# Twelve weight-sum transfers moved to later, the order of compression, norm and scores, and a one-column product in front of each run of scores

## The chip, the cores and the metric

The kernel runs on one core of a Trainium2 chip. The metric is the device time of one execution in microseconds. A core has a matrix engine (PE, with its weight loads PEld), a vector engine (DVE), a scalar engine (ACT), a general engine (POOL) and a queue engine for transfers (SP). SP and POOL start the DMA transfers here: SP those that bring weights on the chip, POOL those of which the change moves twelve.

## The reference

One layer of a hybrid decoder, 256 positions, model width 2048, everything fp32. Three mixers work side by side on one projection; the attention shares queries between a compressed, a selected and a window branch.

```python
h = rms_norm(x, norm_mix_pre)
a_in, b_in, q, kv, nsa_g, merge_g = split(h @ w_in)          # 2048 x 13872
y_a = silu(layer_norm(causal_conv31(a * sigmoid(g)))) @ w_a_out
y_b = (u * (tril(W_s) @ layer_norm(v) + b)) @ w_b_out        # chunks of 128
kc = silu(blocks(k_cmp) @ w1_k) @ w2_k                       # 15 blocks, the same for vc
o = g0 * softmax(q @ kc) @ vc + g1 * softmax(q @ k_slc) @ v_slc + g2 * softmax(q @ k_win) @ v_win
y_c = o @ w_c_out                                            # 16 heads of 64
g_a, g_b, g_c = split(sigmoid(merge_g))
x = x + rms_norm((g_a * y_a + g_b * y_b + g_c * y_c) @ w_o, norm_mix_post)
u_g, u_v = split(causal_conv3(rms_norm(x, norm_ffn_pre) @ w_up))   # 2 x 5632
x = x + rms_norm((silu(u_g) * u_v) @ w_down, norm_ffn_post)
```

With 256 positions there are four key blocks, so the selected branch takes all of them, and the window of 512 masks nothing but the future: both are causal attention over all positions, with keys and values of their own.

## The kernel before, in words

All weights stream from memory, most as pieces of 512 KB. `fetch` starts a piece's transfer on SP into one of five buffers `wraw`. `piece` then splits it: ACT writes the rounded part `whi` (line 199), DVE the rest `wlo` (line 200), four buffers each. A product with such weights is three products, `hi`·`hi`, `hi`·`lo` and `lo`·`hi` (lines 249 to 251 in `mm_t`; lines 228 and 235 for the feature-major projections; line 1056 in class `Seven`).

The order of the program is: projections `a`, `b`, `c` and `q`; `branch()`, which for each of four column blocks `cb` of 512 columns forms gates `pg` from eight pieces of `wt_g` and then the product `py` from four pieces of `wt_p`, and leaves `mac`; `outs_a()`, the same for the first mixer (product `py`, result `ya`); gates and output in `Seven`, which replaces seven of eight products by sums of weights; and the FFN, whose loop also uses sums.

The sums of weights are made in memory by transfers that POOL starts, `ahead`: copies and additions between DRAM buffers. The list `steps` holds them in order. `ahead_by(mark, n)` copies one column of a result of the main line into `tick`, so POOL waits for that result, and then starts the next `n` steps:

```python
        pooled(G.tensor_copy, tick, mark)
        for dst, src, how in steps[:n]:
            pooled(G.dma_start, dst, src, **how)
        del steps[:n]
```

Whatever `n` leaves over, later calls take; the FFN loop spreads what is left over its 42 passes.

Smaller work stands in generators in a queue `bg`: the norm of the first mixer (`lna_gen`, `lnz_gen`: lines 601 to 606, tiles `lz`, `lg`, `At`), the compression of keys and values (`cmp_prep`, `cmp_gen`: `bk`, `zp`, `zs`, `hp`; w1 comes as four pieces for each of the two), and the attention (`cmp_attn` and eight `Unit`s: scores `s` at line 854, weights, transposes `pp`, products into `O`, result `Ct`, whose rest is line 933). `pump(ns)` runs this queue for a budget of nanoseconds between parts of the main line; `hold("outputs")` lets the compression begin at the second block of gates. `in_turn` takes one step of each of its generators in turn, `apart` doubles what a step counts for, and `until(name)` runs the queue to a mark.

Products write to PSUM: four banks hold the main line's results, and four the generators', handed out in turn by `bank`. A run of scores fills two banks, one for each half of the 128 rows (64 rows a head), and takes the halves alternately; `in_turns` makes each product follow the one before it on PE, though others may come between. These products are fp32, and the trace has two records for each.

A scheduler with a simulated timeline of its own sets the final order on every engine, within `tc.issue_after` (this one after that one) and `tc.high_priority` (this one earlier than its place in the program).

Of the kernel before, what the change touches and what calls it, by code (L numbers as in the profile page):

```python
# [64 lines left out]
def block(ctx: ExitStack, tc: tile.TileContext, x, xf, x0, fp, cst, rows, sgw, w1, w2, wf_a, wt_bv, wf_bu, wf_c,  # L65
# [688 lines left out]
        while name not in marks:  # L754
            yield debt[0]

    for kv in range(2):
        bg.append(cmp_prep(kv))
        if kv == 0:
            bg.append(hold("outputs"))  # L760
        bg.append(cmp_gen(kv))

    kkv = s8([128, 2, 1024], F32, "kkv")
    kk = kkv[:, 0].rearrange("p (g b t) -> p g b t", g=2, b=2)
    for i in range(4):
        pc = ftile(wf_c[4 + i], hT)
        fsum(pc, kk[:, i % 2, i // 2], rb=rb)
        ahead_by(kk[:, i % 2, i // 2, 0:1], 1)
        pump(BUDGET)
    vsw = kkv[:, 1].rearrange("p (t c) -> p t c", t=2)  # L770
    gsg = P1.tile([128, 2, 48], F32, name="gsg")
# [22 lines left out]
    for i in range(8):  # L794
        pq = ftile(wf_q[i], hT)
        fsum(pq, qf[:, i], scale=0.125, rb=rb)
        ahead_by(qf[:, i, 0:1], 2 + i % 2)
        pump(BUDGET)


# [2 lines left out]
    def apart(work):  # L803

        for ns in work:
            yield 2.0 * ns
# [39 lines left out]
    def in_turns(work):  # L846


        last = None
        for out, lhsT, rhs, start, stop in work:  # L850
            with ExitStack() as order:
                if last is not None:
                    order.enter_context(tc.issue_after(last))
                last = PE.matmul(out, lhsT=lhsT, rhs=rhs, start=start, stop=stop, skip_group_check=True).ins  # L854

    half = [slice(0, 64), slice(64, 128)]

    class Unit:
# [8 lines left out]
        def scores(self):  # L867
            qt, gg, br = self.at
            nk = (qt + 1) * 128
            mk = cs[:, K_MK + 256 - nk:K_MK + 256]  # L870
            hpb = 512 // nk
            ep = s8([128, 2, 4, 256], F32, f"ep{self.nm}")
            e = self.e = [ep[:, r] for r in range(2)]
            m = self.m = P1.tile([128, 2, 8], F32, tag="am", bufs=2, name="am" + self.nm)
            for b in range(4 // hpb):
                ps = [bank([128, hpb, nk], f"s{self.nm}{b}{r}") for r in range(2)]
                in_turns([(ps[r][:, jj], qf[half[r], gg * 4 + b * hpb + jj, qt * 128:qt * 128 + 128],
                           kk[half[r], gg, br, 0:nk], True, True) for jj in range(hpb) for r in (1, 0)])
                for jj in range(hpb):
                    j = b * hpb + jj  # L880
                    for r in range(2):
                        V.tensor_tensor_reduce(e[r][:, j, 0:nk], ps[r][:, jj], mk, 1.0, -3e38, ALU.add, ALU.max,
                                               m[:, r, j:j + 1])
                        yield nk * 1.05 + 130
            V.tensor_scalar(m[:, :, 0:4], m[:, :, 0:4], -1.0, None, op0=ALU.mult)
# [92 lines left out]
    def attn():  # L978

        units = [Unit(qt, gg, br) for qt in (1, 0) for gg in range(2) for br in range(2)]  # L980
        yield from in_turn(lnz_gen(), apart(cmp_attn(1)), apart(units[0].scores()))
        marks.add("A")
        Ct_box["t"] = s16(P1, [128, 8, 2, T], R, "Ct")
        for n, u in enumerate(units):
            if n + 1 < len(units):
                if n == 1:
                    yield from in_turn(apart(cmp_attn(0)), units[n + 1].scores())
                else:
                    yield from units[n + 1].scores()
            if u.at[2] == 0:  # L990
                V.tensor_mul(spread, pct[u.at[0]][:, u.at[1]][:, None, :].to_broadcast([128, 4, 128]),
                             cs[:, K_RJ:K_RJ + 4][:, :, None].to_broadcast([128, 4, 128]))
            yield from u.weights()
            if SUMS_AT <= n < SUMS_AT + 4:
                yield from input_sums(n - SUMS_AT)
            if u.at[2] == 0:
                O = bank([128, 4, 128], "O" + u.nm)
            yield from u.values(O)
# [149 lines left out]
    def branch():  # L1148

        for cb in range(4):  # L1150
            pg = [PS.tile([128, 512], F32, tag="acc", name=f"pg0{cb}{t}") for t in range(2)]
            for q in range(4):
                hs = granule(wt_g[cb * 4 + q])
                for k in range(4 * q, 4 * q + 4):
                    hi, lo = hs[(k % 4) // 2]
                    c = slice((k % 2) * 512, (k % 2) * 512 + 512)
                    for t in range(2):
                        ts = slice(t * 128, t * 128 + 128)
                        with ExitStack() as order:
                            if (cb, k) == (1, 0):  # L1160
                                order.enter_context(tc.issue_after(norm["v"]))
                            mm_t(pg[t], hT[:, k, 0, ts], hT[:, k, 1, ts], hi[:, c], lo[:, c], k == 0, k == KT - 1)
                if (cb, q) == (0, 2):
                    until("m")
                    debt[0] = 0.0
                elif q < 3:
                    if (cb, q) == (1, 2):
                        marks.add("outputs")
                    pump(BUDGET)
            tgs = {}  # L1170
            for t in range(2):
                for a in range(2):
                    tgs[t, a] = q1(f"mg0{cb}{t}{a}")
                    with tc.high_priority(offset=int(PR)):
                        gated[0] = S.activation(tgs[t, a], pg[t][:, a * 256:a * 256 + 256], AF.Tanh,
                                                scale=rh[:, t:t + 1]).ins
            marks.add("gates")
            pump(BUDGET)
            py = [PS.tile([128, 512], F32, tag="acc", name=f"py0{cb}{t}") for t in range(2)]
            for q in range(2):  # L1180
                hs = granule(wt_p[cb * 2 + q])
                if cb == 0 and q == 0:
                    until("B")
                act = Bt_box["t"]
                for k in range(4 * q, 4 * q + 4):
                    hi, lo = hs[(k % 4) // 2]
                    c = slice((k % 2) * 512, (k % 2) * 512 + 512)
                    for t in range(2):
                        ts = slice(t * 128, t * 128 + 128)
                        with ExitStack() as order:  # L1190
                            if (cb, k) == (0, 7):
                                until("v")
                                debt[0] = max(debt[0], 0.0)
                                order.enter_context(tc.issue_after(norm["v"]))
                            pe_last[0] = mm_t(py[t], act[:, k, 0, ts], act[:, k, 1, ts], hi[:, c], lo[:, c], k == 0, k == 7)
                if q == 0:
                    pump(BUDGET)
            for t in range(2):
                for a in range(2):
                    cc = slice(cb * 512 + a * 256, cb * 512 + a * 256 + 256)  # L1200
                    y = mac[:, t, cc]
                    with tc.high_priority(offset=int(PR)):
                        V.scalar_tensor_tensor(y, tgs[t, a], 1.0, py[t][:, a * 256:a * 256 + 256], op0=ALU.add,
                                               op1=ALU.mult)
            ahead_by(mac[:, 0, cb * 512:cb * 512 + 1], (8, 8, 8, 8)[cb])
            pump(BUDGET)

    def outs_a():

        for cb in range(4):  # L1210
            py = [PS.tile([128, 512], F32, tag="acc", name=f"py1{cb}{t}") for t in range(2)]
            for q in range(2):
                hs = granule(wt_p[(4 + cb) * 2 + q])
                if cb == 0 and q == 0:
                    until("A")
                for k in range(4 * q, 4 * q + 4):
                    hi, lo = hs[(k % 4) // 2]
                    c = slice((k % 2) * 512, (k % 2) * 512 + 512)
                    for t in range(2):
                        ts = slice(t * 128, t * 128 + 128)  # L1220
                        pe_last[0] = mm_t(py[t], At[:, k, 0, ts], At[:, k, 1, ts], hi[:, c], lo[:, c], k == 0, k == 7)
                if q == 0:
                    pump(BUDGET)
            for t in range(2):
                with tc.high_priority(offset=int(PR)):
                    V.tensor_copy(ya[:, t, cb * 512:cb * 512 + 512], py[t])
            if cb < 2:
                ahead_by(ya[:, 0, cb * 512:cb * 512 + 1], (8, 4)[cb])
            pump(BUDGET)

    def m_sums(n):
# [772 lines left out]
```

## Time and the profile before

| | us |
|---|---|
| median of 3 runs | 1563.44 (1559.46 to 1569.31) |
| profiled execution, its own time | 1563.63 |
| its span in the trace | 1561.9 |
| PE busy | 1551.4 (99%) |
| DVE busy | 1322.3 (85%) |
| ACT busy | 970.2 (62%) |
| POOL busy | 220.9 (14%) |
| mean granted clock of PE | 0.998 |

Times below are microseconds from the start of the span. The gates of block 0 begin at about 302; `mac` of the four blocks is ready at 335.1, 377.5, 426.7 and 470.5, when POOL's `tick` copies run; the first two of `outs_a` follow at 495.8 and 517.6. A busy PE is not PE at its peak: the ends of products are modelled, and the distance from one product to the next tells more than the length of one.

### The profile page before, as it was taken

Reading aid. Unit: us, or ns where it says so; the run is one execution under the profiler, and the core shown is the slowest. Engines: PE = TensorE matmul, PEld = TensorE weight load, DVE = VectorE, ACT = ScalarE, POOL = GpSimd, SP = SyncE. Lnnn points to the kernel's source line nnn. Section 1 sums busy time; section 2 is a strip of 40 time slices with the busy share of each in tenths; the row PEclk is TensorE's granted clock in tenths of the full one; section 3 lists DMA queues with packets and bytes.
Section 4 is the critical chain, followed back from the end, with each engine's and each line's share of the span. In section 5 each row is a group of like instructions: output and inputs, shape, how many; then the busy total and the mean of one; then the engine's idle time right before and its main releaser. Section 6 shows DMA issues by size and latency. Waiting matters only on the chain.

```text
span 1561.9 us, 23350 instructions
## 1 busy us (share of the span) xinstructions
PE 1551.4 (99%) x8101; PEld 1315.6 (84%) x8101; DVE 1322.3 (85%) x2233; ACT 970.2 (62%) x1536; POOL 220.9 (14%) x349
## 2 busy tenths in 40 slices
PE   9999999999999999999999999999999999999998
PEld 8888889887777778888888888888888888888887
DVE  7899999876766579978886898888888887899898
ACT  7644454455677776656665766566666666577774
POOL 1011351221102100000000032222222221100000
PEclk9999999999999999999999999999999999999999
DMA  9687998999779867777774699999999999989896
GB/s 369 195 268 234 273 300 246 296 303 288 236 215 256 223 230 262 247 227 259 268 256 164 205 301 309 306 335 290 287 280 283 282 284 281 316 287 346 313 375 218
DMA packets 130711, 426.13 MB, mean 273 GB/s; under 512 B 15008, under 2 KB 16784, under 8 KB 129824
## 3 DMA queue, kind: packets, MB, share of 16 engines
q1 hardware_dynamic: 99648, 329.46, 60.2%
q0 software_dynamic: 30368, 94.52, 25.7%
q8 instruction: 63, 1.03, 0.3%
q10 hardware_dynamic: 576, 0.66, 0.1%
q14 instruction: 56, 0.46, 0.1%
HBM read 416.45 MB, written 90.44 MB: 325 GB/s over the span
## 4 chain that ended last, share of the span: by engine, by line
PE 97%; DMA 1%; DVE 1%; ACT 1%; issue 0%; DVEq 0%; ACTq 0%
PE ps L228 29%; PE ps L235 15%; PE pg L1056 8%; PE pd1a L1056 4%; PE pd0b L1056 4%; PE pd0a L1056 3%; PE pd1b L1056 3%; PE py L250 3%; PE py L251 3%; PE py L249 3%; PE poa L1056 2%; PE pg L251 1%; PE pg L250 1%; PE pg L249 1%; PE s L854 1%; PE po L249 1%
## 5 line engine op out<-in xcount | busy, mean ns | idle before, releaser
L200 DVE TENSOR_TENSOR wlo<-wraw,whi 128x1024 fp32r<-128x1024 f32 (+1 forms) x344 | 418.2, 1221 | 92.3 <-ACT whi L199 73.3
L199 ACT ACTIVATE whi<-wraw 128x1024 fp32r<-128x1024 f32 (+1 forms) x344 | 361.8, 1057 | 212.0 <-PE ps L228 117.8
L228 PE MATMUL ps<-h2T,whi 128*128 128x512 f32 x1360 | 317.2, 390 | 0.0
L228 PEld LDWEIGHTS ps<-h2T,whi 128*128 128x128 f32 x1360 | 252.4, 188 | 50.4
L235 PEld LDWEIGHTS ps<-h2T,wlo 128*128 128x128 f32 x1360 | 169.4, 192 | 3.6
L235 PE MATMUL ps<-h2T,wlo 128*128 128x256 f32 x1360 | 170.7, 283 | 0.0
L228 PE MATMUL ps<-hT,whi 128*128 128x512 f32 x640 | 151.9, 390 | 0.0
L228 PEld LDWEIGHTS ps<-hT,whi 128*128 128x128 f32 x640 | 117.9, 188 | 23.0
L1012 DVE TENSOR_TENSOR wlowraw<-wraw,whiwraw 128x1024 fp32r<-128x1024 f32 x74 | 89.7, 1222 | 26.6 <-ACT whiwraw L1012 24.6
L556 DVE SCALAR_TENSOR_TENSOR cv<-hb,fps,cv 128x256 f32<-128x256 f32 x240 | 105.9, 491 | 0.1
L1012 ACT ACTIVATE whiwraw<-wraw 128x1024 fp32r<-128x1024 f32 x74 | 77.9, 1059 | 40.4 <-PE py L251 11.8
L1615 ACT ACTIVATE fa<-fs,fps 128x256 f32<-128x256 f32 x88 | 52.8, 600 | 54.1 <-DVE fs L274 52.3
L235 PEld LDWEIGHTS ps<-hT,wlo 128*128 128x128 f32 x640 | 81.1, 191 | 2.5
L235 PE MATMUL ps<-hT,wlo 128*128 128x256 f32 x640 | 82.8, 283 | 0.0
L1056 PE MATMUL pg<-whiwraw,hT 128*128 128x512 f32 x256 | 82.3, 395 | 0.0
L129 POOL DMA_DIRECT2D ahead<-in_wt_dq_dram x91 | 68.1, 901 | 87.1 <-DMA ahead<-in_wt_dq_dram 87.1
L129 POOL DMA_DIRECT2D ahead<-ahead x53 | 43.5, 822 | 245.4 <-DMA ahead<-in_wt_dq_dram 103.8
L271 ACT ACTIVATE t<-ps 128x256 f32<-128x256 f32 x125 | 47.5, 382 | 49.0 <-PE ps L235 26.3
L129 POOL COPY tick<-gh 128x1 f32<-128x1 f32 x44 | 37.5, 853 | 186.3 <-ACT gh L1623 186.3
L1056 PEld LDWEIGHTS pg<-whiwraw,hT 128*128 128x128 f32 x256 | 47.9, 188 | 10.4 <-issue 0.2
L1616 DVE SCALAR_TENSOR_TENSOR fa<-fs,fps,fa 128x255 f32<-128x255 f32 x88 | 42.4, 481 | 16.6 <-ACT fa L1615 16.5
L272 DVE TENSOR_TENSOR t<-ps,t 128x256 f32<-128x256 f32 x125 | 52.4, 420 | 0.5 <-ACT t L271 0.5
(2520 smaller groups left out, 3317.9 us busy)
## 6 DMA issues: line engine op xcount, KB each, us to landing
wraw<-in_wf_up_dram SPq DMA_DIRECT2D x176, 512.0 KB, 6.6
ahead<-in_wt_dq_dram POOLq DMA_DIRECT2D x74, 512.0 KB, 9.8
wraw<-in_wt_p_dram SPq DMA_DIRECT2D x48, 512.0 KB, 6.4
wraw<-in_wt_dq_dram SPq DMA_DIRECT2D x33, 512.0 KB, 6.0
wraw<-in_wf_a_dram SPq DMA_DIRECT2D x32, 512.0 KB, 5.1
ahead<-in_wt_gq_dram POOLq DMA_DIRECT2D x32, 512.0 KB, 9.9
wraw<-in_wt_g_dram SPq DMA_DIRECT2D x32, 512.0 KB, 7.1
wraw<-in_wt_gp_dram SPq DMA_DIRECT2D x32, 512.0 KB, 4.9
```

The source lines that it names most:

```text
L129: in_pool[:] = [op(*args, **kw).ins]
L199: S.activation(hi[:, :n], raw[:, :n], AF.Copy)
L200: V.tensor_sub(lo[:, :n], raw[:, :n], hi[:, :n].bitcast(F32))
L228: ins = PE.matmul(ps, lhsT=ws[k // 8][0][:, c:c + 128], rhs=mov[:, k], start=bool(k == 0 and first), stop=bool(k == n - 1 and not first), ...
L235: ins = PE.matmul(ps[:, 1], lhsT=ws[k // 8][1][:, c:c + 128], rhs=mov[:, k, 0], start=bool(k == 0 and not first), stop=bool(k == n - 1 and ...
L249: PE.matmul(ps, lhsT=xh, rhs=hi, start=first, stop=False)
L250: PE.matmul(ps, lhsT=xh, rhs=lo, start=False, stop=False)
L251: return PE.matmul(ps, lhsT=xl, rhs=hi, start=False, stop=last).ins
L556: V.scalar_tensor_tensor(ca[:, j], hb[:, j, k:k + T], w(j, k), ca[:, j], op0=ALU.mult, op1=ALU.add)
L1012: seq[eng] = [op(*args, **kw).ins]
L1056: ins = PE.matmul(bank, lhsT=a[x], rhs=w[y], start=first and j == 0, stop=bool(last and j == 2), skip_group_check=more).ins
L1615: S.activation(a, s, AF.Identity, bias=fps[:, C_FB + f:C_FB + f + 1], scale=w[2])
```

## The change

It has three parts.

1. The counts of `ahead_by` change. After each of the four `kk` projections none are started (before: 1 each); after the eight `q` projections 2 each (before: 2 and 3 alternately); after block 0 of `branch` 4 (before 8); in `outs_a` 8, 8 and 4 after the first three blocks (before 8 and 4 after the first two). By the end of block 0 twelve fewer have been started; `outs_a` takes up eight of them and the FFN loop four (108 there, before 104).
2. The second `cmp_gen` leaves the queue and is taken in turn with the norm and the scores of the first unit; `cmp_attn(1)`, which was in turn with these two, follows behind them.
3. In front of each run of scores stands a product of one column into the bank of half 0. It is written over by the run's own product. The banks are asked for in the other order, and the rest of the run follows it at high priority.

```diff
-    for kv in range(2):
-        bg.append(cmp_prep(kv))
-        if kv == 0:
-            bg.append(hold("outputs"))
-        bg.append(cmp_gen(kv))
+    bg.append(cmp_prep(0))
+    bg.append(hold("outputs"))
+    bg.append(cmp_gen(0))
+    bg.append(cmp_prep(1))
...
         fsum(pc, kk[:, i % 2, i // 2], rb=rb)
-        ahead_by(kk[:, i % 2, i // 2, 0:1], 1)
...
-        ahead_by(qf[:, i, 0:1], 2 + i % 2)
+        ahead_by(qf[:, i, 0:1], 2)
...
                 if last is not None:
                     order.enter_context(tc.issue_after(last))
+                    order.enter_context(tc.high_priority(offset=int(PR)))
...
-                ps = [bank([128, hpb, nk], f"s{self.nm}{b}{r}") for r in range(2)]
-                in_turns([(ps[r][:, jj], qf[half[r], gg * 4 + b * hpb + jj, qt * 128:qt * 128 + 128],
+                ps = [bank([128, hpb, nk], f"s{self.nm}{b}{r}") for r in (1, 0)][::-1]
+                in_turns([(ps[0][:, 0, 0:1], qf[half[0], gg * 4, 0:128], kk[half[0], gg, br, 0:1], True, True)]
+                         + [(ps[r][:, jj], qf[half[r], gg * 4 + b * hpb + jj, qt * 128:qt * 128 + 128],
                            kk[half[r], gg, br, 0:nk], True, True) for jj in range(hpb) for r in (1, 0)])
...
-        yield from in_turn(lnz_gen(), apart(cmp_attn(1)), apart(units[0].scores()))
+        yield from in_turn(cmp_gen(1), lnz_gen(), apart(units[0].scores()))
+        yield from cmp_attn(1)
...
-            ahead_by(mac[:, 0, cb * 512:cb * 512 + 1], (8, 8, 8, 8)[cb])
+            ahead_by(mac[:, 0, cb * 512:cb * 512 + 1], (4, 8, 8, 8)[cb])
...
-            if cb < 2:
-                ahead_by(ya[:, 0, cb * 512:cb * 512 + 1], (8, 4)[cb])
+            if cb < 3:
+                ahead_by(ya[:, 0, cb * 512:cb * 512 + 1], (8, 8, 4)[cb])
```

Three places in the order of instructions show what this moves. The numbers behind the names of tiles count buffers and differ between the two programs. First PE, at the last run of scores of a unit, before the change: `s` are the scores, `py` a product of the second mixer, `Bt` its operand.

```order
L251 MATMUL py_4348<-whi_4482,Bt 128x512
L854 MATMUL s_4401<-kkv,qf 128x256
L249 MATMUL py_4349<-whi_4482,Bt 128x512
L250 MATMUL py_4349<-wlo_4483,Bt 128x512
L251 MATMUL py_4349<-whi_4482,Bt 128x512
L854 MATMUL s_4400<-kkv,qf 128x256
L854 MATMUL s_4401<-kkv,qf 128x256
L854 MATMUL s_4400<-kkv,qf 128x256
```

One product of the run stands apart from its other three, with three 512-column products between them. The same engine after the change, at a run of the first units; line 853 is the line 854 of before, and `pcp` is the transpose in `cmp_attn`.

```order
L837 MATMUL pcp_4330<-idn,ce_4318 128x128 x2
L853 MATMUL s_4339<-kkv,qf 128x1
L853 MATMUL s_4338<-kkv,qf 128x256
L853 MATMUL s_4339<-kkv,qf 128x256
L853 MATMUL s_4338<-kkv,qf 128x256
L853 MATMUL s_4339<-kkv,qf 128x256
L853 MATMUL s_4350<-kkv,qf 128x1
```

The four products stand together behind their one-column product; so they do in all twelve runs, and the claim of the next run stands behind them here. Two of the twelve claims stand alone among 512-column products.

Second ACT, at the gates of block 2, before: the `whi` at line 199 are the splits of weight pieces.

```order
L694 ACTIVATE bk_3926<-bt_3942 128x4x64
L199 ACTIVATE whi_4043<-wraw_4041 128x1024
L199 ACTIVATE whi_4049<-wraw_4047 128x1024
L199 ACTIVATE whi_4079<-wraw_4077 128x1024
L199 ACTIVATE whi_4143<-wraw_4141 128x1024
L199 ACTIVATE whi_4149<-wraw_4147 128x1024
L199 ACTIVATE whi_4208<-wraw_4206 128x1024
L199 ACTIVATE whi_4214<-wraw_4212 128x1024
L716 ACTIVATE zs_4091<-zp_3947 128x256
L716 ACTIVATE zs_4092<-zp_3947 128x256
```

And the same stretch of ACT after the change.

```order
L199 ACTIVATE whi_4040<-wraw_4038 128x1024
L694 ACTIVATE bk_3910<-bt_3926 128x4x64
L603 ACTIVATE lg_3996<-lz_3995 128x256
L601 ACTIVATE lz_4027<-cv,fps 128x256
L603 ACTIVATE lg_4028<-lz_4027 128x256
L601 ACTIVATE lz_4088<-cv,fps 128x256
L199 ACTIVATE whi_4046<-wraw_4044 128x1024
L603 ACTIVATE lg_4089<-lz_4088 128x256
L601 ACTIVATE lz_4147<-cv,fps 128x256
L199 ACTIVATE whi_4076<-wraw_4074 128x1024
L605 ACTIVATE At<-lz_3995 128x256
L605 ACTIVATE At<-lz_4027 128x256
```

Norm operations (`lz`, `lg`, `At`) now stand among the splits; before, the norm came behind `zs`.

Third POOL, from the `tick` of block 0 of `branch` on, before: the `bt` are buffers of the compression.

```order
L129 COPY tick<-mac 128x1
L129 DMA ahead_80<-ahead_80 128x512
L129 DMA ahead_81<-in_wt_gq_dram 128x512
L129 DMA ahead_81<-in_wt_gq_dram 128x1024
L129 DMA ahead_82<-in_wt_gq_dram 128x1024
L687 MEMSET bt_3589 128x16
L687 MEMSET bt_3594 128x16
L687 MEMSET bt_3599 128x16
L687 MEMSET bt_3604 128x16
L129 DMA ahead_81<-ahead_81 128x512
L129 DMA ahead_82<-in_wt_gq_dram 128x512
```

POOL after the change, from the second transfer behind the same `tick` to the `tick` of block 1.

```order
L129 DMA ahead_79<-in_wt_gq_dram 128x512
L129 DMA ahead_79<-in_wt_gq_dram 128x1024
L129 DMA ahead_80<-in_wt_gq_dram 128x1024
L687 MEMSET bt_3577 128x16
L687 MEMSET bt_3582 128x16
L687 MEMSET bt_3587 128x16
L687 MEMSET bt_3592 128x16
L687 MEMSET bt_3911 128x16
L687 MEMSET bt_3916 128x16
L687 MEMSET bt_3921 128x16
L687 MEMSET bt_3926 128x16
L129 COPY tick<-mac 128x1
```

Of the eight transfers behind the first `tick` four are left, and the buffers of both compressions follow at once. The `tick` of block 1 has eight behind it before and after.

At the end of the attention, the last unit's product into `O` stood among the first products of `Seven` (`pg0s`); after the change it stands eleven products ahead of them.

## The prediction

> **What bounds the kernel now.** First the page: the span, the busy shares, the largest wait of the transfer queue, and the landing times of two weight streams.
>
> ```profile
> span 1561.9 us, 23350 instructions
> PE 1551.4 (99%) x8101; PEld 1315.6 (84%) x8101; DVE 1322.3 (85%) x2233; ACT 970.2 (62%) x1536; POOL 220.9 (14%) x349
> L129 POOL COPY tick<-gh 128x1 f32<-128x1 f32 x44 | 37.5, 853 | 186.3 <-ACT gh L1623 186.3
> wraw<-in_wt_p_dram SPq DMA_DIRECT2D x48, 512.0 KB, 6.4
> wraw<-in_wt_g_dram SPq DMA_DIRECT2D x32, 512.0 KB, 7.1
> ```
>
> PE is busy in 99% of the span. The diff takes no product away, so it can only gain where PE stands still or runs slowly. I therefore cut the span into stretches (columns: us, PE busy, PEld, DVE, ACT, POOL, granted clock, DMA share, GB/s).
>
> ```profile
> 300.00:320.00 20.00, 20.00 (x90) 16.56 (x89) 13.37 (x22) 8.78 (x9) 5.92 (x11) 1.00 1.03 319
> 360.00:380.00 20.00, 17.69 (x94) 14.53 (x95) 14.67 (x23) 15.29 (x23) 2.10 (x5) 1.00 0.87 312
> 380.00:400.00 20.00, 18.65 (x82) 15.19 (x82) 11.18 (x15) 8.40 (x12) 3.63 (x6) 0.91 0.99 296
> 395.50:398.80 3.30, 3.30 (x9) 2.62 (x8) 3.19 (x7) 3.06 (x5) 0.03 (x1) 0.50 1.11 324
> 400.00:560.00 160.00, 160.00 (x798) 119.47 (x798) 104.13 (x297) 119.20 (x303) 20.05 (x32) 1.00 0.79 225
> 560.00:580.00 20.00, 18.89 (x84) 13.41 (x84) 14.65 (x16) 13.07 (x16) 0.00 (x0) 1.00 0.60 188
> ```
>
> PE stands still for 2.31 us in 360 to 380, 1.35 in 380 to 400 and 1.11 in 560 to 580, and runs 3.3 us at half clock. Between 400 and 560 it never stops. The weight loads' waits name the places; first those of 340 to 400, last that of 540 to 600 (us in total, times, longest).
>
> ```profile
> PEld py L249 <- ACT whi L199: 2.1, 2, 1.1
> PEld hp L720 <- ACT zs L716: 1.8, 1, 1.8
> PEld py L250 <- DVE wlo L200: 1.0, 1, 1.0
> PEld pg L250 <- DVE wlo L200: 1.0, 1, 1.0
> PEld pg0s L1056 <- DVE Ct L933: 1.5, 1, 1.5
> ```
>
> A weight load waits while the product before it still streams, so each wait costs PE a product's pitch less. That pitch is 389.74 to 389.96, taken as 0.23 us:
>
> ```profile
> 389.74 0.39 PE L251 MATMUL pg<-whi,hT 128*128 128x512 f32 x1
> 389.96 0.39 PE L249 MATMUL pg<-whi,hT 128*128 128x512 f32 x1
> 393.51 1.16 PE L720 MATMUL hp<-sel,zs 128*128 128x64 f32 x8 [1.35 <-ACT zs L716]
> 396.35 0.63 PE L249 MATMUL pg<-whi,hT 128*128 128x512 f32 x1
> 396.77 0.63 PE L250 MATMUL pg<-wlo,hT 128*128 128x512 f32 x1
> ```
>
> - **A**, `py` of column block 1 (blocks count from 0) waiting for split weights: 2.1 + 1.0 - 3 x 0.23 = 2.4 us.
> - **B**, `pg` for `wlo`: 1.0 - 0.23 = 0.8.
> - **C**, `hp` for `zs`: 1.8 - 0.23 = 1.6. Behind it the clock halves: the pitch is 0.42 (396.35 to 396.77), so the 3.3 us hold the work of 3.3 x 0.23 / 0.42 = 1.8 and lose 1.5; with the edges I take 1.7.
> - **D**, the first lump behind attention for `Ct`: 1.5 - 0.23 = 1.3.
>
> Together 7.8 us, 0.5% of the span.
>
> **The change part by part.** *Fewer transfers before 400 us.* The chain of the first two rows gives the late weight pieces; the others are POOL's issues beside them.
>
> ```profile
> 352.94 9.74 DMA wraw<-in_wt_p_dram
> 380.87 11.16 DMA wraw<-in_wt_g_dram
> 350.38 0.81 POOL L129 DMA_DIRECT2D ahead<-ahead  x1 [7.37 <-issue]
> 352.92 0.80 POOL L129 DMA_DIRECT2D ahead<-in_wt_oq_dram  x1
> 378.94 2.00 POOL L129 DMA_DIRECT2D ahead<-in_wt_oq_dram  x3
> ```
>
> The `wt_p` piece takes 9.74 us against a median of 6.4, and starts with POOL's transfers of 350 to 353. These are the second four of column block 0's eight, which the change drops; the twelve that it has dropped by then also leave POOL less behind. I take A as gone: -2.4 (0 to -2.4). B's piece and C's come behind block 1's tick, whose eight stay, and the 11.16 us piece is issued 2 us behind three of them. The backlog that they meet is shorter, so I take half of B, -0.4, and two thirds of C, -1.0 (each from 0 to all). The half clock stands behind C's stop and a run of 64-column products, and goes if that stop is short: -1.3 (0 to -1.7).
>
> [...]
>
> *Later transfers.* Eight come back behind the second and third of `outs_a`'s blocks (about 495 to 555), four in the FFN. The nearest row is 300 to 320: DMA share 1.03, and PE still 20.00 of 20.00; 400 to 560 has 0.79. So 0, at worst another A: +2.4. In the FFN POOL's tick waits 186.3 us for `gh` in all; four more issues of 0.8 us fit there. Without that cover they would be 4 x 0.8 = 3.2 us of POOL, which no product waits for until the sums are read.
>
> *One-column products.* Score runs that are split cost more than whole ones:
>
> ```profile
> 404.81 0.70 PE L854 MATMUL s<-kkv,qf 64*128 64x256 f32 x2
> 405.43 0.50 PE L251 MATMUL pg<-whi,hT 128*128 128x512 f32 x1
> 407.47 1.13 PE L854 MATMUL s<-kkv,qf 64*128 64x256 f32 x6
> 408.52 0.50 PE L250 MATMUL pg<-wlo,hT 128*128 128x512 f32 x1
> 462.31 1.13 PE L854 MATMUL s<-kkv,qf 64*128 64x256 f32 x8
> 463.37 0.50 PE L251 MATMUL py<-whi,Bt 128*128 128x512 f32 x1
> ```
>
> Split: 0.62 + 1.05 = 1.67; whole: 1.06; difference 0.6. Six of the twelve runs are split in the order of before, and the pitches give 3.3 us in all; after the change all twelve stand whole: -3.3 (0 to -3.3, since some of that may only move). Each has a product of one column more, ten next to its run or other 64-row products, two alone. The nearest row has one-column products of 128 rows:
>
> ```profile
> 43.84 0.50 PE L436 MATMUL ssp<-ones,sq 128*128 128x1 f32 x4
> 44.20 0.49 PE L249 MATMUL pv<-swraw,hT 128*128 128x512 f32 x1
> ```
>
> Four records are two fp32 products, 0.36 us: 0.18 each, 12 x 0.18 = +2.2. The lower end is 0, since its one column may pass under the weight load of the next product; the upper end is the price of a whole product of the run, 1.06 / 4 = 0.27 each, 3.2. I take 0.18, a product of the same one column. The two alone cost a change to 64 rows and back, by the split run 0.6 / 3 = 0.2 each: +0.4. The step comes to -0.7, between -3.3 (claims and switches free) and +3.6 (dear claims, and no split saved).
>
> [...]
>
> *The order of compression, norm and scores.* The first norm operations now stand on ACT ahead of weight splits of block 2's gates (the order shown above), where before only splits stood.
>
> ```profile
> 382.36 1.06 ACT L199 ACTIVATE whi<-wraw 128x1024 fp32r<-128x1024 f32 x1 [2.58 <-PE pg L251]
> 388.81 1.06 ACT L199 ACTIVATE whi<-wraw 128x1024 fp32r<-128x1024 f32 x1 [5.39 <-PE pg L251]
> 392.13 1.06 ACT L199 ACTIVATE whi<-wraw 128x1024 fp32r<-128x1024 f32 x1 [2.25 <-DMA wraw<-in_wt_g_dram]
> 396.82 0.59 ACT L601 ACTIVATE lz<-cv,fps 128x256 f32<-128x256 f32 x1
> 399.25 0.42 ACT L605 ACTIVATE At<-lz 128x256 fp32r<-128x256 f32 x1 [0.33 <-DVE lz L604]
> ```
>
> Ten operations of 0.42 to 0.59 us are 4 x 0.5 + 2 x 0.5 + 4 x 0.42 = 4.7 us. They are covered by ACT's idle time in 380 to 393, 2.58 + 5.39 + 2.25 = 10.2 us. But they wait for DVE between one another, and the split behind them, and PE behind it, wait too. With full cover 0, without any 4.7, with a second half clock 6.4; nearest is the cover: I take **+1.5**. At the end of attention the last bank's product now stands 11 products (2.5 us) ahead of the first lump, where before it stood among them; D's 1.3 us fits: -1.1 (0 to -1.3).
>
> **Sum.** -2.4 - 0.4 - 1.0 - 1.3 - 1.1 - 0.7 + 1.5 = -5.4. From the profiled execution, 1563.63 us, which stands 0.2 above the median of the runs: **1558.2 us**.
>
> **Rivals.** *The burst behind block 1 decides.* C and the half clock hang on the eight transfers at 377 to 381 alone, which stay; for it speaks the 11.16 us row, against it the shorter backlog. Then B's -0.4, C's -1.0 and the clock's -1.3 are out: 1558.2 + 2.7 = 1560.9.
>
> *Slower: norm operations hold the splits.* The ten ACT operations queue in the stretch where PE has two pieces in hand. Decisive is that ACT's 10.2 us idle come in three pieces, each waiting for `pg` or a landing: if the operations fall outside them, 4.7 us reach PE, and the 1.7 of a second half clock. C and the half clock stay. Kept are A's -2.4, D's -1.1 and the -0.7: 1563.6 - 4.2 + 6.4 = 1565.8. Against it: the cover is twice the work.
>
> *The change doesn't relieve the queue.* `wt_p` at 352.94 is late through the compression's pieces and its own granules, not through POOL. For it: 300 to 320 holds a DMA share of 1.03 without a stop. Then A, B, C and the clock stay, -0.7 and -1.1 stand against +1.5: 1563.3.
>
> **How the numbers follow.** Forecast 0.45, burst 0.25, slower 0.14, no relief 0.13, anything else 0.03. The gains at their bounds (2.4 + 0.8 + 1.6 + 1.7 + 1.3 + 3.3) are 11.1, so the low end is 1552; the high end takes in the second rival and 1 us of the later transfers: 1567. A measurement here tells 1%, 15.6 us, from no change; all stops together are half of that, so faster by over 1% has 0.02, and slower by it, which needs more than the second rival's whole price, 0.03.
>
> **What would show it.** A right: between 355 and 370 no `py` waits for `whi` or `wlo`, and no `wt_p` piece takes over 8 us there. C right: `hp` waits less than 0.6 us and no stretch has 0.50. The claims right: each 64-row run whole, and a run of five products at most 1.3 us. Rival two shows as `pg` of block 2 waiting for `whi` with ACT busy on `lz`, `lg` or `At` just before. I am wrong if new stops of over 3 us stand in 400 to 560, where before there are none, or if the FFN waits for its sums.

## The result and the profile after

The changed kernel takes 1555.07 us (median of 8 executions, 1554.56 to 1556.31); the kernel before, measured beside it, 1566.56 (8 executions, 1559.46 to 1571.14). The ratio is 0.9933, with a 95% interval of 0.9915 to 0.9951: faster by 0.7%. The time lies inside the range of the prediction; the gain is about twice what was forecast from the profiled executions, of which more below. Two things changed at once: the median fell by 11.5 us, and the spread went from 11.7 us to 1.8.

The profiled execution after took 1556.31 us, 7.3 below the profiled one of before. First the page, with the rows that were shown of before.

```profile
span 1554.6 us, 23403 instructions
PE 1547.9 (100%) x8125; PEld 1316.0 (85%) x8125; DVE 1322.2 (85%) x2233; ACT 968.7 (62%) x1536; POOL 230.6 (15%) x346
wraw<-in_wt_p_dram SPq DMA_DIRECT2D x48, 512.0 KB, 6.1
wraw<-in_wt_g_dram SPq DMA_DIRECT2D x32, 512.0 KB, 6.1
```

PE has 24 more matmul records (two for each of the twelve claims) and is busy for 3.5 us less in a span that is 7.3 us shorter: it stands still 3.8 us less, and none of the stretches below runs at half clock. The same stretches as before (us, PE, PEld, DVE, ACT, POOL, granted clock, DMA share, GB/s):

```profile
360.00:380.00 20.00, 20.00 (x110) 16.93 (x109) 15.78 (x33) 16.25 (x31) 3.04 (x6) 1.00 0.77 238
380.00:400.00 20.00, 19.72 (x107) 16.37 (x105) 15.20 (x34) 13.57 (x27) 2.69 (x4) 1.00 1.03 321
400.00:560.00 160.00, 160.00 (x813) 119.40 (x812) 99.52 (x268) 113.54 (x285) 25.37 (x41) 1.00 0.83 240
560.00:580.00 20.00, 20.00 (x90) 16.52 (x89) 19.60 (x23) 14.90 (x17) 0.00 (x0) 1.00 0.86 286
```

The 2.31, 1.35 and 1.11 us of standing in 360 to 380, 380 to 400 and 560 to 580 are 0, 0.28 and 0, and the clock is 1.00 in all four. Weight loads that wait (first of 340 to 400, then of 400 to 600):

```profile
PEld hp L720 <- ACT zs L716: 0.7, 1, 0.7
PEld pg L1057 <- DVE Ct L933: 0.2, 1, 0.2
```

No `py` and no `pg` waits for `whi` or `wlo`. `hp` still waits 0.7 - 0.23 = 0.5 us for `zs`, and behind it the pitch is that of the full clock:

```profile
390.47 1.15 PE L720 MATMUL hp<-sel,zs 128*128 128x64 f32 x8 [0.28 <-ACT zs L716]
393.17 0.39 PE L251 MATMUL pg<-whi,hT 128*128 128x512 f32 x1
393.40 0.40 PE L250 MATMUL pg<-wlo,hT 128*128 128x512 f32 x1
```

POOL, from block 0's `tick` to block 1's, and then the transfers issued in 350 to 360, among them block 1's four `wt_p` pieces: the share of the DMA engines by queue, and the median time to landing.

```profile
335.55 0.18 POOL L129 COPY tick<-mac 128x1 f32<-128x1 f32 x1 [21.22 <-DVE mac L1204]
336.68 2.18 POOL L129 DMA_DIRECT2D ahead<-in_wt_gq_dram  x3
374.06 0.18 POOL L129 COPY tick<-mac 128x1 f32<-128x1 f32 x1 [6.06 <-DVE mac L1204]
...
q1 hardware_dynamic: 815, 2.97, 85.4%
wraw<-in_wt_p_dram SPq DMA_DIRECT2D x4, 512.0 KB, 5.3
```

The same place before:

```profile
335.06 0.18 POOL L129 COPY tick<-mac 128x1 f32<-128x1 f32 x1 [4.67 <-DVE mac L1203]
339.13 0.82 POOL L129 DMA_DIRECT2D ahead<-ahead  x1 [3.89 <-DMA ahead<-in_wt_gq_dram]
...
q0 software_dynamic: 389, 1.14, 53.7%
q1 hardware_dynamic: 521, 1.88, 49.2%
wraw<-in_wt_p_dram SPq DMA_DIRECT2D x4, 512.0 KB, 10.3
```

Ahead of block 0's `tick` POOL now idles for 21.22 us, where before it idled for 4.67 and then had another transfer to wait for: its backlog is gone. It starts nothing between 339 and 374, so the four of 350 to 353 are missing. Before, their queue (q0) and that of the weight pieces (q1) held the DMA engines for about half the time each; after, q0 has nothing in this stretch, and block 1's `wt_p` pieces land in 5.3 us in place of 10.3.

### The profile page after: what moved, and what is told of

It is laid out like the page before. It is cut to its first block, busy times and chain, and to the rows that moved or that the text cites. A ratio compares the mean times of both kernels' runs of the same rounds, so it can differ in the third digit from the quotient of the medians.

```text
span 1554.6 us, 23403 instructions
## 1 busy us (share of the span) xinstructions
PE 1547.9 (100%) x8125; PEld 1316.0 (85%) x8125; DVE 1322.2 (85%) x2233; ACT 968.7 (62%) x1536; POOL 230.6 (15%) x346
## 4 chain that ended last, share of the span: by engine, by line
PE 98%; DMA 1%; DVE 1%; ACT 0%; issue 0%; DVEq 0%; ACTq 0%
PE ps L228 29%; PE ps L235 15%; PE pg L1057 8%; PE pd1a L1057 4%; PE pd0b L1057 4%; PE pd0a L1057 3%; PE pd1b L1057 3%; PE py L249 3%; PE py L251 3%; PE py L250 3%; PE poa L1057 2%; PE pg L251 2%; PE pg L250 2%; PE pg L249 2%; PE s L853 1%; PE po L250 1%
## 5 line engine op out<-in xcount | busy, mean ns | idle before, releaser
L129 POOL COPY tick<-gh 128x1 f32<-128x1 f32 x44 | 36.8, 837 | 178.7 <-ACT gh L1624 178.7
L1057 PEld LDWEIGHTS pg<-whiwraw,hT 128*128 128x128 f32 x256 | 47.9, 188 | 11.5 <-issue 1.6
```

Of the source, the lines that this page charges most:

```text
L129: in_pool[:] = [op(*args, **kw).ins]
L1057: ins = PE.matmul(bank, lhsT=a[x], rhs=w[y], start=first and j == 0, stop=bool(last and j == 2), skip_group_check=more).ins
```

## The experiments

The parts of the change can be built apart. With part 1 alone the order of PE, ACT and DVE is row for row that of before; with parts 2 and 3 alone it is row for row that of the changed kernel.

**Each part alone, and the kernel before again.** The edit of the first:

```diff
-        ahead_by(kk[:, i % 2, i // 2, 0:1], 1)
-        ahead_by(qf[:, i, 0:1], 2 + i % 2)
+        ahead_by(qf[:, i, 0:1], 2)
-            ahead_by(mac[:, 0, cb * 512:cb * 512 + 1], (8, 8, 8, 8)[cb])
+            ahead_by(mac[:, 0, cb * 512:cb * 512 + 1], (4, 8, 8, 8)[cb])
-            if cb < 2:
-                ahead_by(ya[:, 0, cb * 512:cb * 512 + 1], (8, 4)[cb])
+            if cb < 3:
+                ahead_by(ya[:, 0, cb * 512:cb * 512 + 1], (8, 8, 4)[cb])
```

> Part 1 alone: the twelve transfers moved, the order of compression, norm and scores and the score runs as before; PE's and ACT's order is that of before row for row. Theory Q (the stops of 340 to 400 come from POOL's transfers in front of the weight pieces): A, B, most of C and the half clock go, 2.4 + 0.7 + 1.1 + 1.7 = 5.9 us against before's profile; D (the wait for Ct, 1.3) and the split runs stay; and since these stops are also what differs from run to run, the median falls by 7 to 9 us against before's median and the runs lie within 3 us of each other. Theory O (they come from the compression's own weight pieces and from hp behind the splits, which part 2 moves): within 1 us of before, with its spread of some 10 us.

Measured: 1557.22 us (1556.60 to 1557.76) against 1564.64 of before (23 executions, 1560.89 to 1572.33), ratio 0.9945 (0.9926 to 0.9963). Its waits in 340 to 400, then in 540 to 600, and its stretches from 360:

```profile
PEld hp L720 <- ACT zs L716: 0.6, 1, 0.6
PEld pg0s L1055 <- DVE Ct L932: 1.5, 1, 1.5
...
360.00:380.00 20.00, 20.00 (x110) 17.31 (x109) 16.20 (x24) 12.97 (x19) 3.05 (x6) 1.00 0.79 244
380.00:400.00 20.00, 19.81 (x106) 16.54 (x105) 9.71 (x17) 9.68 (x15) 2.69 (x4) 1.00 1.04 330
```

Theory Q holds: on the same order of instructions A, B, most of C and the half clock are gone, D is still there, and the spread is 1.2 us. Theory O falls. So does the prediction's first rival: the eight transfers behind block 1's `tick` are all there (373.59 to 390), and `hp` waits 0.6 - 0.23 = 0.4 us with them.

```diff
+    bg.append(cmp_prep(0))
+    bg.append(hold("outputs"))
+    bg.append(cmp_gen(0))
+    bg.append(cmp_prep(1))
...
-        yield from in_turn(lnz_gen(), apart(cmp_attn(1)), apart(units[0].scores()))
+        yield from in_turn(cmp_gen(1), lnz_gen(), apart(units[0].scores()))
+        yield from cmp_attn(1)
```

> Part 2 alone: cmp_gen(1) in turn with the norm and the first scores, cmp_attn(1) behind; transfers and score runs as before. Theory Q: A stays (2.4 us of py of block 1 waiting for whi and wlo), B, C and the half clock depend on the burst and stay too; D goes, since the last product into O now stands 17 products ahead of the first lump: 1 to 2 us faster than before's median, with its spread. Theory O: 6 to 9 us faster than before's median, spread under 3 us.

Measured: 1563.30 us (12 executions, 1560.79 to 1568.82), ratio 0.9988 (0.9972 to 1.0004). It isn't told apart from no change. `py` of block 1 still waits for its weights, `hp` for `zs`, and the clock halves behind it; no wait for `Ct` is left.

```profile
PEld py L249 <- ACT whi L199: 3.9, 3, 1.7
PEld hp L720 <- ACT zs L716: 2.0, 1, 2.0
...
398.80:402.20 3.40, 3.40 (x12) 2.24 (x11) 2.71 (x5) 2.70 (x6) 0.00 (x0) 0.51 1.06 321
```

The waits are as theory Q expects.

```diff
-                ps = [bank([128, hpb, nk], f"s{self.nm}{b}{r}") for r in range(2)]
+                ps = [bank([128, hpb, nk], f"s{self.nm}{b}{r}") for r in (1, 0)][::-1]
-                in_turns([(ps[r][:, jj],
+                in_turns([(ps[0][:, 0, 0:1], qf[half[0], gg * 4, 0:128], kk[half[0], gg, br, 0:1], True, True)]
+                         + [(ps[r][:, jj],
```

The high priority goes with it; added to parts 1 and 2 alone (built, not run) it leaves the order of every engine as it is.

> Part 3 alone: the one-column product and the high priority; transfers and the order of generators as before. Theory Q and O alike: A, B, C, the half clock and D stay. By the prediction's terms whole runs save 3.3 us, less what stays split here, and the claims cost 2.2 + 0.4: -0.7, between -3.3 and +3.6 against before's median, with its spread. A rival (the claims are the real gain): 5 us or more faster.

Measured: 1563.01 us (12 executions, 1560.54 to 1568.59), ratio 0.9991 (0.9977 to 1.0006): not told apart from no change; A is there (`py` waits 3.6 us for `whi` in two places), and so is D. The claims are not the gain.

> The kernel before once more, nothing changed, for a second trace of it. Theory Q: its stops stand in 340 to 400 again but with other lengths, up to 8 us more or 4 us less in all than the 7.4 of the first trace, and the rest of the span is the same to 1 us. A rival (the spread of before is spread over the whole span, so no stop explains it): 340 to 400 the same to 1 us, and the difference elsewhere.

Measured: 1562.75 us, one execution. Waits of its 340 to 400, and one of 220 to 262:

```profile
PEld py L249 <- ACT whi L199: 1.9, 2, 1.1
PEld hp L720 <- ACT zs L716: 0.9, 1, 0.9
...
PEld ps L228 <- ACT whi L199: 0.6, 1, 0.6
```

The same places, other lengths: `hp` waits 0.9 in place of 1.8, and the clock stays at 1.00. And there are new places: projections around 230 and 250 wait for weights, where the first trace shows none, and PE stands for 0.52 us at 405.67 (scores waiting for DVE) and for 0.60 at 809.25 (a product waiting for a split piece). So each of the two expectations holds in part: the stops of 340 to 400 change from one execution to the next, but some of the change lies elsewhere. No trace of an execution above 1565 us was taken, so what its 7 us more consist of isn't shown.

**Each part left out.** Without the claims (parts 1 and 2):

> The changed kernel without part 3 (parts 1 and 2). Claims pay: by the terms -3.3 + 2.2 + 0.4 it is 0.7 slower than the changed kernel, at about 1555.8. Claims don't pay, since the order of part 2 alone already takes D away and the traces put a claim at 2.6 us in all: 0 to 1.5 us faster than the changed kernel, 1553.5 to 1555.

Measured: 1554.52 us (1554.36 to 1556.01), against 1555.07 and 1554.81 of the two measurements of the changed kernel. The claims bring nothing that can be measured: the medians are 0.3 to 0.6 us apart, and the ranges overlap. Without them five of the twelve runs are split.

> The changed kernel without part 2 (parts 1 and 3). D is back (the lump behind attention waits 1.3 us or more for Ct): 1 to 2 us slower than the changed kernel, 1556 to 1557.5, with its small spread. If part 2 also mattered for hp in 380 to 400, hp waits over 0.6 us there.

Measured: 1556.55 us (1555.66 to 1557.35), 1.5 to 1.7 above the changed kernel. D is back:

```profile
PEld pg0s L1057 <- DVE Ct L934: 2.0, 1, 2.0
```

2.0 - 0.23 = 1.8 us, which is the whole worth of part 2. `hp` waits 0.9 here, 0.4 to 0.7 in the changed kernel, the counts alone and the one without claims, and not at all in the second trace of the changed kernel: too close to put it down to part 2.

> The changed kernel with the counts of before (parts 2 and 3). Theory Q: A, B, C and now and then the half clock are back in 340 to 400, the spread is 8 us or more again, and the median is 6 to 8 us above the changed kernel, 1561 to 1563. The rival (the three parts help each other, and any two do most): within 3 us of it.

Measured: 1561.55 us (12 executions, 1558.91 to 1568.67), beside 1562.48 of before (20 executions), ratio 0.9993 (0.9977 to 1.0010). With parts 2 and 3 in place and the old counts, nearly all of the gain is gone and the spread is back.

```profile
PEld hp L720 <- ACT zs L716: 1.4, 1, 1.4
PEld py L249 <- ACT whi L199: 1.1, 1, 1.1
```

**The price of a claim.**

```diff
-                in_turns([(ps[0][:, 0, 0:1], qf[half[0], gg * 4, 0:128], kk[half[0], gg, br, 0:1], True, True)]
+                in_turns([(ps[0][:, 0, 0:1], qf[half[0], gg * 4, 0:128], kk[half[0], gg, br, 0:1], True, True)] * 5
```

> The changed kernel with five one-column products in front of each run in place of one: 48 more. [...] The order of a few other instructions shifts with them, by 1 us at most.

Measured: 1565.24 us (7 executions, 1563.91 to 1567.60). Above the changed kernel's 1555.07 that is 10.2 us for 48 products: 0.21 us each. The trace agrees: a run with its claim takes 1.29 us on PE (374.38 to 375.67) where a run without one took 1.06.

```profile
374.38 1.35 PE L853 MATMUL s<-kkv,qf 64*128 64x1 f32 x10
375.67 0.39 PE L709 MATMUL zp<-whi,bk 128*128 128x256 f32 x1
```

At that price twelve claims are 12 x 0.21 = 2.5 us. The prediction's 0.18, from one-column products over 128 rows, would have made it 48 x 0.18 = 8.6 us for the 48 and 2.2 for the twelve.

The weight loads show what one claim costs. First five claims in a row, of the kernel with five; then a whole run of eight 128-column products, and a claim that stands alone, both of the changed kernel:

```profile
483.89 1.19 PEld L853 LDWEIGHTS s<-kkv,qf 64*128 64x128 f32 x10 [0.81 <-DVE vbd L992]
...
531.41 0.97 PEld L853 LDWEIGHTS s<-kkv,qf 64*128 64x128 f32 x16 [0.35 <-issue]
...
436.69 0.40 PE L249 MATMUL pg<-whi,hT 128*128 128x512 f32 x1
437.02 0.38 PE L853 MATMUL s<-kkv,qf 64*128 64x1 f32 x2
437.33 0.51 PE L250 MATMUL pg<-wlo,hT 128*128 128x512 f32 x1
```

The ten loads of five claims start (1.19 - 0.19) / 9 = 0.11 us apart, with 0.19 for one load, two for each product: 0.22 us, the measured price. A run alternates between the two halves of the rows, and in the trace its 16 loads start in pairs, the two of a pair 0.01 us apart or less and the pairs 0.11: eight products in 0.97 us, less than the 1.19 of five claims. The claims stand all on one half; that this is why they take longer is an estimate from these rows, since no run puts them on both. A claim alone takes 0.31 us to the next product (437.02 to 437.33), and the product ahead of it, at 0.33, takes 0.10 more than the pitch of 0.23.

**Which of the twelve matter.** Only block 0's count (8 to 4, and `outs_a` 8, 8), on the kernel before:

> The kernel before with one count changed: 4 in place of 8 after block 0 of branch (the other four go to the second block of outs_a). Theory Q as the prediction had it (A comes from the second four, started at 350 to 353): A and most of C go, 5 to 7 us below before's median, with a spread under 4 us. If the backlog of the projections matters as well: only 2 to 4 us, and the spread stays above 5.

Measured: 1558.79 us (10 executions, 1557.33 to 1560.93), beside 1561.41 of before (26 executions), ratio 0.9980 (0.9971 to 0.9989). Only the projections' eight fewer, with 8 behind block 0:

> The kernel before with the eight fewer of the kk and q projections, and 8 after block 0 as before (outs_a takes the eight). Theory Q as the prediction had it: the second four still start in the flight of block 1's wt_p pieces, A stays: 0 to 2 us below before's median, spread above 5. If the backlog decides: 4 us or more.

Measured: 1561.38 us (11 executions, 1559.35 to 1563.43), ratio 0.9998 (0.9989 to 1.0007). Both have the order of before on PE, ACT and DVE, row for row. Waits of block 0 only in 300 to 400 and in 220 to 262 (first two rows), then of projections only in 300 to 400; with each, the landing of block 1's four `wt_p` pieces (issued in 350 to 360):

```profile
PEld hp L720 <- ACT zs L716: 0.5, 1, 0.5
PEld ps L228 <- ACT whi L199: 1.1, 1, 1.1
wraw<-in_wt_p_dram SPq DMA_DIRECT2D x4, 512.0 KB, 5.4
...
PEld py L249 <- ACT whi L199: 1.9, 2, 1.1
PEld pg L250 <- DVE wlo L200: 1.0, 1, 1.0
PEld hp L720 <- ACT zs L716: 0.9, 1, 0.9
wraw<-in_wt_p_dram SPq DMA_DIRECT2D x4, 512.0 KB, 8.6
```

Block 0's four are what A and B hang on, and most of C: with them out, the `wt_p` pieces land in 5.4 us and `py` waits nowhere; with the other eight out alone they take 8.6, and A, B and C stay, A and C shorter than in the first trace. All six traces of kernels with these four show a `py` of 340 to 400 waiting for a split piece, and none of the eight without them. The clock halved in two of those six. But the time fell by 2.6 us, not by the 5 to 7 that were expected of these four alone; 2 to 4 were expected if the projections' transfers matter as well. The wait that block 0 only has left stands at 251 us, behind the `kk` projections, whose four transfers it still has; of the six traces with those four, three show a stop there, and of the eight without them none. Both sets out, as in the counts alone, gave 1557.2, 1.6 below block 0 alone, though on another chip; that the `kk` transfers make this difference is a reading of such rows, not tried by itself.

**A further step.** Without the claims, and 4 behind block 1 as well:

> Parts 1 and 2 without the claims, and 4 in place of 8 after block 1 (outs_a 8, 8, 8). Rival one of the prediction (the burst behind block 1 decides what is left): the 0.4 us of hp's wait goes, 0.3 to 0.6 below the kernel without claims, 1 us below the changed kernel. Otherwise as without claims, 0.5 below the changed kernel.

Measured: 1558.26 us (11 executions, 1557.38 to 1560.41), 3.5 above the changed kernel. Nothing of what was hoped for: `hp` waits as in the changed kernel, and `Ct` is late again. The last two rows are block 2's four `wt_p` pieces (issued in 380 to 400), here and without claims.

```profile
PEld hp L720 <- ACT zs L716: 0.7, 1, 0.7
PEld pg0s L1055 <- DVE Ct L931: 2.0, 1, 2.0
wraw<-in_wt_p_dram SPq DMA_DIRECT2D x4, 512.0 KB, 5.7
...
wraw<-in_wt_p_dram SPq DMA_DIRECT2D x4, 512.0 KB, 11.1
```

So the burst behind block 1 does lengthen the pieces that it meets, from 5.7 to 11.1 us, as block 0's lengthened block 1's. But without claims, with pieces of 11.1 us, no product of block 2 waits for a split: they are slow and still in time. The new count also shifted the order on PE, ACT and DVE in many places, among them the last product into `O`, which stands among the first `pg0s` again. So 1.8 of the 3.5 us is D; whether the rest is the later transfers or the order stays open, and the run doesn't test the count cleanly.

> The changed kernel once more, for a comparison on the same chip: 1555.1, within 1 us, and a trace in which 340 to 400 has less than 1 us of stops.

Measured: 1554.81 us (1554.61 to 1555.40), beside 1561.41 of before: ratio 0.9956 (0.9944 to 0.9969). In 340 to 400 PE is busy for 60.00 of 60 us. The changed kernel and the one without claims are the fastest of all versions; their ranges overlap, and they were not timed beside one another, so neither is shown to be the better.

## Why the prediction was right, and where its sizes were off

The direction, the range and the mechanism held: the gain comes from stops that POOL's transfers cause in front of weight pieces. Point by point, from the two profiled executions and the runs above:

- **A** was forecast to go and went, 2.4 us. The reason was right in detail: the four transfers of 350 to 353 (block 0 alone takes A away, the projections alone don't), through the landing of the pieces beside them (10.3 us with them, 5.3 without).
- **B, C and the half clock** were forecast at a half, two thirds and three quarters of their size (-2.7). They went nearly in full: 0.8 + 1.1 + 1.7 = 3.6. The step that held them back, the burst behind block 1, has no such weight: it is there in the changed kernel and in the counts alone. Why B and C go together with A isn't taken apart: the `wt_g` piece that was named for them is issued behind the first four of that burst in both traces (380.87 before, 379.80 after). The sign for C, `hp` waiting less than 0.6 us, is met only if the pitch is taken off its 0.7; in the second trace of the changed kernel it waits for nothing.
- **D** was forecast at -1.1 and is -1.3, and it is part 2's doing, since the order alone removes it and the changed kernel without part 2 has it.
- **The order's +1.5** is 0. The norm operations do stand between splits on ACT, and ACT still waits for pieces and for PE's release behind them:

```profile
379.66 1.07 ACT L199 ACTIVATE whi<-wraw 128x1024 fp32r<-128x1024 f32 x1 [0.77 <-PE pg L251]
389.08 1.06 ACT L199 ACTIVATE whi<-wraw 128x1024 fp32r<-128x1024 f32 x1 [0.99 <-DMA wraw<-in_wt_g_dram]
```

  The cover that was argued from ACT's idle time held, and its end, 0, was the better choice. The second rival, which rested on this, fell with it: no `pg` of block 2 waits for a split.
- **The score step's -0.7** is -0.2: from each score product to the next product on PE, the traces have 16.6 us in all before and 16.3 after (15.6 with parts 1 and 2, without claims, so the claims lose what part 2's order had saved). The saving by whole runs was near: by the same sums some 3.3 us. The price of the claims was mis-sized: 2.2 + 0.4 was forecast, with ten claims beside their run or other 64-row products, and the trace has 5 x 0.22 + 0.12 + 6 x 0.31 = 3.1: five claims stand directly ahead of their run, one behind the run before, and six apart from any score product, as at 437.02. Nor do all twelve runs stand whole after the change, as was said with it: products into `O` still cut the one at 494 us. The sign for the claims holds for the runs of five products (1.29 us).
- **Later transfers** were taken at 0, and are: PE is busy for 160.00 of 160 us in 400 to 560 with a DMA share of 0.83, and POOL's idle time before `gh` in the FFN is 178.7 us, against 186.3.

The terms as measured, -2.4 - 3.6 - 1.3 - 0.2 = -7.5, are close to the 7.3 us between the two profiled executions. The remaining step that failed is the base. I summed from one profiled execution and took its 0.2 us above the median of three for a sign that it stood for the kernel. Four medians of before are 1566.6, 1564.6, 1562.5 and 1561.4, and those of the changed kernel 1555.1 and 1554.8: the difference is 11.5 us in the first pair and 6.6 in the last, and it is the kernel before that moves. The second median is from one chip, the last two are from another, and for the first the chip isn't known; how much of the movement is the chip isn't shown. Three executions with a spread of 10 us should have said that the stops in the trace are one draw of lengths that change. From the four medians the same gain of 5.4 would have given 1556.0 to 1561.2, so how near 1558.2 came to 1555.07 is in part luck.

The third rival, that the transfers don't matter, is ruled out by the counts alone.

## What to carry to other kernels

Where a kernel's executions differ by 10 us and its trace shows a few late weight pieces, the lateness may be the variable part: take away the transfers that start in the flight of those pieces. Here the counts alone took the spread from 11.4 us to 1.2 and the median down by 7.4. Background transfers are best judged by when they start beside the pieces that the main engine waits for next, not by their number and not by how much they slow a piece: four of them alone were worth 2.6 us, eight others alone nothing that could be measured, and those behind block 1 made pieces twice as slow that no product waited for. A product that only claims a bank has a price too, and here it cost at least what it saved.

## What the runs showed of the hardware

A product of one column over 64 rows in fp32 cost 0.21 us in a row of its like, all on one half of the rows. In runs that alternate between the halves, eight 128-column products took 1.09 us, 0.14 each, and four 256-column products 1.06, 0.27 each, so one column was not cheaper than 128. The ten loads of five such claims, two for a product, took 1.19 us and started 0.11 apart; the 16 loads of the run of eight took 0.97 and started in pairs.

Four 256 to 512 KB transfers of POOL, between DRAM buffers, in the flight of four 512 KB weight pieces doubled the time of those, 10.3 us against 5.3 in the changed kernel, and 5.4 with these four alone left out; those behind block 1 did the same to block 2's pieces, 11.1 against 5.7.

Away from the first and last microseconds of each trace, the clock halved twice in the fourteen traces, for 3.4 us each time (the mean granted clock is 0.998 in these two executions and 0.999 or 1.000 in the other twelve), and both times behind a stop of `hp` followed by its eight 64-column records: 1.35 us of idle PE in the first trace of before, 1.52 in the order alone. It did not halve behind stops of 1.44 and 1.52 us that wide products followed, in the claims alone and without the order:

```profile
397.22 1.16 PE L720 MATMUL hp<-sel,zs 128*128 128x64 f32 x8 [1.52 <-ACT zs L716]
...
362.42 0.74 PE L249 MATMUL py<-whi,Bt 128*128 128x512 f32 x2 [1.44 <-ACT whi L199]
...
560.45 0.50 PE L1057 MATMUL pg0s<-whig00r,hT 128*128 128x512 f32 x1 [1.52 <-DVE Ct L934]
```

Whether the narrow products make this difference is not shown: no run varied them. In the clock's record of the first trace of before the half clock lasts 3.413 us, and the stretches at full clock ahead of it and behind it are 114 and 340 such lengths; what sets these lengths isn't shown.
